# A two-layer diffusion block on one core: a running maximum spread to all partitions through DRAM, and two pieces of work moved to later steps

## The chip, the cores and the metric

The kernel runs on one core of a Trainium2 chip. The metric is the device time of one execution in microseconds; the number given for a kernel is the median of its runs. The profile is one further execution recorded by the hardware profiler. [...]

## What is computed

Two layers work on 256 latent tokens and 256 context tokens of width 1024, all in float32. Layer 0 mixes tokens with a convolution module (a depthwise convolution of 31 taps between two pointwise products), layer 1 with a bidirectional mLSTM of 4 heads of width 512. Each is followed by a squared-ReLU MLP of width 4096, and each sublayer ends in a layer norm of `ALPHA*x + gate*F(x*(1+scale)+shift)`. Only the latent tokens are the output. What matters here of the mLSTM is how its weights are made stable:

```python
bcum = jnp.cumsum(lfc, axis=-1)
dlog = bcum[..., :, None] - bcum[..., None, :] + ic[..., None, :]
dlog = jnp.where(lower, dlog, -jnp.inf)
inter = bcum + m[..., None]
m_row = jnp.maximum(inter, jnp.max(dlog, axis=-1))
scores = jnp.einsum('bhtd,bhsd->bhts', qc, kc) * jnp.exp(dlog - m_row[..., None])
...
den = jnp.sum(scores, axis=-1) + w_inter * jnp.einsum('bhtd,bhd->bht', qc, n)
h = num / jnp.maximum(jnp.abs(den), jnp.exp(-m_row))[..., None]
```

The kernel doesn't scan over chunks: it writes the whole as attention over the 512 tokens, with weights `exp(a_s + negm_t) * S`, where `a = i - bcum` and `negm` is minus the running maximum of `a`.

## The kernel before, in words

One program, written in a framework that takes instructions in program order, gives earlier ones priority, simulates the engines and from that fixes the order on each engine and queue, with all semaphores. `tc.issue_after(x)` puts what is traced in its block behind instruction x on the same engine. A tile of a tag with n buffers waits until the oldest tile of that tag has been read for the last time.

Products of weights and activations are done in three matmuls, with both operands split into a high and a low part (`mm3` and `mm3t`, lines 179 to 213). Weights come by DMA into one of three buffers `raw` (`raw_load`, line 141, on SP's queue) and are split by ScalarE (line 149, `wh`) and VectorE (line 150, `wl`) into a ring of `NW` = 4 blocks. Results of products lie in PSUM tiles, in rings by tag: "mm" 3, "ln" 2, "cv" 2, "fl" 1.

Three places are touched.

**The convolution (layer 0).** Columns of `pw1` come out one output at a time (`pw1_next`, line 900, called behind the product of output m). The depthwise convolution of 128 tokens is done as a product with a Fourier table (`fwd`, line 817), products with the transformed taps on VectorE (`products`, lines 843 and 844, into tiles `F`, a ring of 5) and an inverse transform of eight matmuls (`back`, line 854), whose result VectorE adds up with a bias (861) and takes statistics of (862). `whole` (line 809) does all three for one block of tokens; for blocks 2 and 3 it is called at outputs m = 4 and 5, behind the epilogue `pw1_epi` of that output, which ends in four transposes (line 801).

**The end of layer 0's MLP.** The last of four pieces of the second product is done in two passes over the columns of 256 tokens, the latent ones (s = 1) first. Its epilogue `e2` scales a result and adds it to the residual (line 1071, which frees the product's PSUM bank), and calls `feed0(m, s)` (line 1108), which feeds a layer norm. When the eighth part of a pass is in, the norm is finished, and for s = 1 all eight items of `u1_half` (line 1120) are traced at once: each item applies the norm (lines 577 and 578, VectorE), then scale and shift into a high part and a copy (line 600, two on ScalarE) and the low part (line 601, VectorE). The second pass (s = 0) comes behind that. The items' results are first used by the product with `up_z`.

**The mLSTM's heads (layer 1).** `Z.att` (line 44) says how steps of generators are mixed: a main chain (`o0` is the output gate of head 0, 16 steps of 12 matmuls) and a side chain, of which so many steps are taken for each step of the main one. `G0` is `decay` (line 1348): gate sums, their running maximum (the scan at line 1404) as rows `negm` of 36 partitions x 256, two transposes of it on TensorE (line 1410) and from these `guard`, the lower bound of the denominator (lines 1412 and 1414). `W0` to `W3` are `weights` (line 1450), one per head: for each direction d a matmul with a selecting matrix spreads one row of `negm` to all 128 partitions in a PSUM bank "ln" (line 1458); exponentials (lines 1466 and 1472, ScalarE), masks (1470), products with the scores (1473) and sums (1482, 1484) on VectorE give `pw` and `es`. `A0` to `A3` (`attend`) multiply them with the values; before head h's first result is used, `denominators` (line 1488) sums `es` on TensorE (1493) and reads `guard`.

Of the kernel before, what the change touches and what calls it, by code (L numbers as in the profile page):

```python
# [8 lines left out]
F32 = mybir.dt.float32  # L9
# [5 lines left out]
P = 128  # L15
D = 1024
# [15 lines left out]
class Z:  # L32
# [8 lines left out]
    pipeS = 1  # L41
    apsum = 'mm'
    dpsum = 'mm'
    att = [['o0', 'G0 W0 W1', 2], ['o1', 'A0 W2', 1.6], ['o2', 'A1 W3 D0', 2.1], ['o3', 'A2 V3', 1], ['D1 E3 D2', 'A3', 3], ['D3', '', 0]]

# [23 lines left out]
def hybrid_kernel(ctx: ExitStack, tc: tile.TileContext, xT, vecs_d, wdw_d, ada0_w, ada_w, wg_d, pw1a, pw1, pw2, w1_0, w2_0,  # L71
# [28 lines left out]
    def psum(tag="mm"):  # L100
        return pp.tile([P, 512], F32, tag=tag, name=nm(tag), bufs={"mm": 3, "ln": 2, "fl": 1, "cv": 2}[tag])
# [704 lines left out]
            for tt in range(2):  # L806
                whole(tt, [psum() for _ in range(2)])

    def whole(tt, xfs):
        fwd(0, tt, xfs)  # L810
        products(0, tt)
        products(0, tt)
        back(0, tt, psum("cv"))

    ps_ = {}

# [30 lines left out]
    def back(h, tt, o):  # L847
        sl = slice(h * 512, (h + 1) * 512)
        for i, g_ in enumerate((G1, G2)):
            for b in (0, 1):  # L850
                r = 64 * b

                def inv():
                    return nc.tensor.matmul(o[r:r + 64, :], g_[:, r:r + 64], ps_[tt][0][b][i], start=i == 0, stop=i == 1,  # L854
                                            tile_position=(0, r))
                if b == 0:
                    lead = inv()
                else:
                    with tc.issue_after(lead.ins):
                        inv()  # L860
        nc.vector.tensor_tensor(Y[tt][h], o, bdw[:, sl], op=ALU.add)
        nc.vector.bn_stats(bst[:, tt, h, :], Y[tt][h])
# [37 lines left out]
    def pw1_next(m, ps):  # L900
        if m == 3:
            first.extend(ada_load(0, 4))
            ada_g1.mm(first, range(4))
        if m == 11:
            ada_s2.mm(half + ada_load(0, 6 + ada_s2.n, halves=(1,)))
            with tc.issue_after(mark["gate"]):
                nc.scalar.activation(warm, eps, AF.Silu)
        pw1_epi(m + KO0, ps)
        if m in (1, 2):
            taps(m - 1)  # L910
        if m in (4, 6, 8):
            unit = ada_g1 if m == 4 else ada_s2
            blocks = ada_load(0, unit.u0 + unit.n)
            with tc.issue_after(lastmm[0]):
                unit.mm(blocks)
        if m in (4, 5):
            whole(m - 2, [psum(), psum("ln")])
        if m == 5:
            ada_g1.end()
        if m == 8:  # L920
            for i, tag in enumerate("SLSL"):
                half.append(tmp(tag))
                nc.sync.dma_start(half[i], ada_w[0, 6 + ada_s2.n, 0, :, i * 512:(i + 1) * 512])
        if m == 10:
            pw2_raw.extend(raw_load(pw2[g, 0]) for g in range(2))
# [175 lines left out]
            ada_n1.step()  # L1101

    lns = norm_pair(maker(hp, "ln", 3))
    cab1, u1 = [], {}

    AGAIN = [4, 5, 6, 7, 0, 1, 2, 3]

    def feed0(m, s):
        sl = HALVES[s][1]
        lns[s].feed(x[m][:, sl])  # L1110
        if len(lns[s].ts) == DT:
            lns[s].finish()
            if not cab1:
                ada_n1.flush()
                cab1.extend(comb(1, "ln2_g0", "ln2_b0", "sc1", "sh1"))
            if s == 1:
                for _ in u1_half(s):
                    pass

    def u1_half(s):  # L1120
        for i in range(DT):
# [215 lines left out]
    def gcol(d, h):  # L1337
        return 32 * d + h
# [4 lines left out]
    make_lower_triangular(nc, lower)  # L1343
    acol = con.tile([P, 4, NG], F32, name="acol")
    negm = con.tile([NG, C], F32, name="negm")
    guard = con.tile([P, 2, NG], F32, name="guard")

    def decay(_):
        gT = tmp("L")
        nc.scalar.copy(gT, gps)  # L1350
        yield
        gk = psum("ln")
        for b in range(4):
            nc.tensor.matmul(gk[:, b * 16:(b + 1) * 16], gT[:, b * P:(b + 1) * P], foldg, start=True, stop=True)
        gs = tmp("S")[:, 0:64].rearrange("p (b c) -> p b c", b=4)
        nc.vector.tensor_tensor(gs, gk[:, 0:64].rearrange("p (b c) -> p b c", b=4),
                                VA("b_gate").rearrange("p (b c) -> p b c", b=4), op=ALU.add)
        gb_ = [tmp("L"), tmp("E"), tmp("E")]
        g8 = [gb_[i // 3][:, (i % 3) * 4 * NG:(i % 3 + 1) * 4 * NG].rearrange("p (b c) -> p b c", b=4) for i in range(8)]
        ig, fg, bsb, ex, up1, cor, lf, fa = g8  # L1360
        nc.vector.memset(ig, 0.0)
        nc.vector.memset(fg, 0.0)
        for d in range(2):
            nc.vector.tensor_copy(ig[:, :, 32 * d:32 * d + 4], gs[:, :, 8 * d:8 * d + 4])
            nc.vector.tensor_copy(fg[:, :, 32 * d:32 * d + 4], gs[:, :, 8 * d + 4:8 * d + 8])


        nc.vector.scalar_tensor_tensor(fa, fg, -1.0, fg, op0=ALU.mult, op1=ALU.max)
        nc.scalar.activation(ex, fa, AF.Exp, scale=-1.0)
        nc.vector.tensor_scalar(up1, ex, 1.0, None, op0=ALU.add)  # L1370
        nc.vector.scalar_tensor_tensor(cor, up1, -1.0, ex, op0=ALU.add, op1=ALU.subtract)
        nc.scalar.activation(lf, up1, AF.Ln)
        nc.vector.reciprocal(up1, up1)
        nc.vector.tensor_tensor(cor, cor, up1, op=ALU.mult)
        nc.vector.tensor_tensor(lf, cor, lf, op=ALU.subtract)
        nc.vector.tensor_scalar(fa, fg, 0.0, None, op0=ALU.min)
        nc.vector.tensor_tensor(lf, lf, fa, op=ALU.add)

        nc.vector.memset(up1, 0.0)
        for d, (b0, b1, b2, b3) in ((0, (0, 1, 2, 3)), (1, (1, 0, 3, 2))):  # L1380
            c = slice(32 * d, 32 if d == 0 else NG)
            nc.vector.tensor_copy(up1[:, b1, c], lf[:, b0, c])
            nc.vector.tensor_tensor(up1[:, b2, c], up1[:, b1, c], lf[:, b1, c], op=ALU.add)
            nc.vector.tensor_tensor(up1[:, b3, c], up1[:, b2, c], lf[:, b2, c], op=ALU.add)
        yield
        yield
        bps = psum("ln")
        for d, cum in ((0, upper), (1, lower)):
            c = slice(32 * d, 32 if d == 0 else NG)
            reg = bps[:, 0:4 * NG].rearrange("p (b c) -> p b c", b=4)[:, :, c]  # L1390
            nc.tensor.matmul(reg, cum, lf[:, :, c], start=True, stop=False)
            nc.tensor.matmul(reg, ones, up1[:, :, c], start=False, stop=True)
        nc.vector.tensor_copy(bsb, bps[:, 0:4 * NG].rearrange("p (b c) -> p b c", b=4))
        nc.vector.tensor_tensor(acol, ig, bsb, op=ALU.subtract)

        yield
        aT = psum("ln")
        for b in range(4):
            nc.tensor.transpose(aT[:NG, b * P:(b + 1) * P], acol[:, b, :], ident)
        aR, mR = tmp("S"), tmp("S")  # L1400
        nc.vector.tensor_copy(aR[:32, :], aT[:32, :])
        nc.vector.tensor_copy(aR[32:NG, LO], aT[32:NG, LO])
        nc.vector.tensor_copy(aR[32:NG, HI], aT[32:NG, T - 1:C - 1:-1])
        nc.vector.tensor_tensor_scan(mR[:NG, :], aR[:NG, :], aR[:NG, :], 0.0, op0=ALU.max, op1=ALU.max)
        nc.vector.tensor_scalar(negm[:32, :], mR[:32, HI], -1.0, None, op0=ALU.mult)
        nc.vector.tensor_scalar(negm[32:NG, :], mR[32:NG, T - 1:C - 1:-1], -1.0, None, op0=ALU.mult)
        yield
        mT = psum("ln")
        for t in range(2):
            nc.tensor.transpose(mT[:, t * NG:(t + 1) * NG], negm[:, t * P:(t + 1) * P], ident[:NG, :NG])  # L1410
        yield
        nc.vector.tensor_tensor(guard, mT[:, 0:2 * NG].rearrange("p (t c) -> p t c", t=2), bsb[:, 2:4, :],
                                op=ALU.subtract)
        nc.scalar.activation(guard, guard, AF.Exp)
# [12 lines left out]
    close_pool()  # L1427
    close_pool()
    qe = open_pool("qe")
    sel = {d * 4 + h: ident[:NG, gcol(d, h):gcol(d, h) + 1].broadcast_to([NG, P]) for d in range(2) for h in range(H)}  # L1430
    mask = qe.tile([P, 2, 2, P], F32, name="mask")
    nc.gpsimd.memset(mask, 0.0)
    nc.gpsimd.tensor_scalar(mask[:, 0, 0, :], upper, -1.0, -NEG, op0=ALU.add, op1=ALU.mult)
# [16 lines left out]
    def weights(h):  # L1450


        es = tmp("F").rearrange("p (d t) -> p d t", d=2) if h % 2 else ES()
        short = PW(F32R)
        for d in range(2):
            cidx = gcol(d, h)
            nb = psum("ln")
            nc.tensor.matmul(nb[:, :C], sel[d * 4 + h], negm, start=True, stop=True)
            yield
            for i, b in enumerate(blocks[d]):  # L1460
                q0, q1 = rng[d, b]
# [233 lines left out]

    def chain(names):
        for n_ in names.split():
            yield from dict(G=decay, W=weights, o=gate_o, V=values, A=attend, D=down, E=early)[n_[0]](int(n_[1]))

    for main, side, per in Z.att:  # L1700
        side = chain(side)
# [268 lines left out]
```

## Time and profile before

| | before |
|---|---|
| median of 3 runs | 1683.69 us (1683.51 to 1685.66) |
| the profiled execution | 1685.65 us, span 1683.9 us |
| granted TensorE clock, mean | 0.998 |
| busy: DVE, ACT, POOL | 61%, 44%, 1% |
| HBM read, written | 283.32 MB, 15.73 MB |

How to read it: the span runs from the first to the last recorded instruction; the profiled execution's own time is 1.75 us longer. Busy shares are averages over the whole span. A matmul's recorded time includes part of its pipeline, so the distance from one start to the next tells what it costs. The chain that ended last follows from the last instruction back what released each.

### The profile page before, as it was taken

What the parts mean: (1) busy time and instruction counts of PE and PEld (TensorE: products, weight loads), DVE (VectorE), ACT (ScalarE), POOL (GpSimd) and SP (SyncE); (2) the same over time, 40 slices, a digit from 0 to 9 for tenths busy, and PEclk for the clock granted to TensorE, in tenths of its full rate; (3) what the DMA queues carried; (4) which work ended last, traced back from release to release, by engine and by line L of the source; (5) the groups of instructions that cost most, each with busy time, mean ns of one, the idle gap of its engine ahead of it and who ended that gap; (6) DMA issues with size and microseconds to landing.
All of it is one profiled execution on the core that took longest, in us unless ns stands there. A gap on an engine that the chain in (4) does not pass through costs nothing.

```text
span 1683.9 us, 22944 instructions
## 1 busy us (share of the span) xinstructions
PE 1670.1 (99%) x8960; PEld 1371.5 (81%) x8960; DVE 1035.3 (61%) x1877; ACT 743.3 (44%) x1197; POOL 14.3 (1%) x64
## 2 busy tenths in 40 slices
PE   9999999999999999999999999999999999999998
PEld 6665898888888998877788899888878878878887
DVE  6555895666635766752143653564478785786677
ACT  4313573232324476652243533442466564555453
POOL 0000000000000000000000000000000000000001
PEclk9999999999999999999999999999999999999999
DMA  9547223444324065556775752455454555675552
GB/s 357 192 150 273 86 75 113 150 137 139 138 100 150 15 200 181 184 192 250 264 257 175 254 183 104 156 188 176 145 191 174 199 216 195 247 282 184 192 180 96
DMA packets 71835, 300.53 MB, mean 178 GB/s; under 512 B 7282, under 2 KB 22386, under 8 KB 41648
## 3 DMA queue, kind: packets, MB, share of 16 engines
q1 hardware_dynamic: 54064, 284.39, 47.7%
q10 hardware_dynamic: 17664, 14.69, 2.6%
q8 instruction: 70, 1.15, 0.3%
q14 instruction: 37, 0.30, 0.1%
HBM read 283.32 MB, written 15.73 MB: 178 GB/s over the span
## 4 chain that ended last, share of the span: by engine, by line
PE 96%; DVE 3%; DMA 1%; issue 0%; ACT 0%; SPq 0%; DVEq 0%
PE mm L180 17%; PE mm L183 17%; PE mm L184 17%; PE mm L195 7%; PE mm L213 4%; PE mm L211 4%; PE mm L212 4%; PE mm L196 4%; PE cv L211 2%; PE cv L212 2%; PE cv L213 2%; PE fl L342 1%; PE cv L854 1%; PE ln L180 1%; PE fl L772 1%; PE ln L183 1%
## 5 line engine op out<-in xcount | busy, mean ns | idle before, releaser
L150 DVE TENSOR_TENSOR wl<-raw,wh 128x1024 fp32r<-128x1024 f32 x344 | 419.0, 1222 | 270.6 <-ACT wh L149 253.4
L149 ACT CAST wh<-raw 128x1024 fp32r<-128x1024 f32 x344 | 358.9, 1051 | 504.1 <-PE mm L183 270.4
L183 PE MATMUL mm<-u,wh 128*128 128x512 f32 (+1 forms) x808 | 292.1, 362 | 0.3 <-DVE u L610 0.2
L180 PE MATMUL mm<-u,wh 128*128 128x512 f32 (+1 forms) x680 | 244.3, 360 | 0.0
L184 PE MATMUL mm<-u,wl 128*128 128x512 f32 (+1 forms) x680 | 241.8, 356 | 0.0
L183 PEld LDWEIGHTS mm<-u,wh 128*128 128x128 f32 x808 | 152.6, 189 | 23.8 <-issue 1.5
L180 PEld LDWEIGHTS mm<-u,wh 128*128 128x128 f32 x680 | 128.4, 189 | 27.4 <-issue 8.8
L184 PEld LDWEIGHTS mm<-u,wl 128*128 128x128 f32 x680 | 128.5, 189 | 18.9 <-issue 1.2
L211 PE MATMUL mm<-wh,xl 128*128 128x512 f32 x256 | 101.5, 397 | 0.0
L212 PE MATMUL mm<-wh,xl 128*128 128x512 f32 x256 | 101.2, 395 | 0.0
L180 PE MATMUL mm<-xm,wh 128*128 128x512 f32 x256 | 101.0, 395 | 0.0
L213 PE MATMUL mm<-wl,xl 128*128 128x512 f32 x256 | 99.9, 395 | 0.2 <-DVE wl L150 0.2
L184 PE MATMUL mm<-xm,wl 128*128 128x512 f32 x256 | 99.7, 390 | 0.0
L180 PE MATMUL mm<-hid,wh 128*128 128x512 f32 (+1 forms) x256 | 93.3, 364 | 1.1 <-DVE x L1071 1.1
L184 PE MATMUL mm<-hid,wl 128*128 128x512 f32 (+1 forms) x256 | 92.8, 363 | 0.0
L183 PE MATMUL mm<-hid,wh 128*128 128x512 f32 (+1 forms) x256 | 92.8, 363 | 0.0
L195 PE MATMUL mm<-x,wh 128*128 128x512 f32 x232 | 81.1, 398 | 0.0
L425 DVE SCALAR_TENSOR_TENSOR S<-ar,cs,S 128x512 f32<-128x512 f32 x56 | 40.8, 749 | 61.1 <-DMA ar<-ada_w 60.9
L183 PE MATMUL mm<-qq,wh 128*128 128x272 f32 x256 | 73.9, 289 | 0.0
L180 PE MATMUL mm<-qq,wh 128*128 128x272 f32 x256 | 73.5, 289 | 0.0
L184 PE MATMUL mm<-qq,wl 128*128 128x272 f32 x256 | 73.5, 288 | 0.0
L195 PE MATMUL mm<-u,wh 128*128 128x512 f32 x192 | 68.7, 399 | 0.0
(535 smaller groups left out, 3278.0 us busy)
## 6 DMA issues: line engine op xcount, KB each, us to landing
raw<-w SPq DMA_DIRECT2D x64, 1024.0 KB, 4.8
raw<-wo SPq DMA_DIRECT2D x32, 1024.0 KB, 4.8
raw<-ada_w SPq DMA_DIRECT2D x24, 1024.0 KB, 6.4
ar<-ada_w SPq DMA_DIRECT2D x80, 256.0 KB, 3.3
raw<-wv SPq DMA_DIRECT2D x16, 1024.0 KB, 6.6
raw<-wqT SPq DMA_DIRECT2D x16, 1024.0 KB, 5.9
raw<-wq SPq DMA_DIRECT2D x16, 1024.0 KB, 5.3
raw<-wk SPq DMA_DIRECT2D x16, 1024.0 KB, 5.1
```

The lines of the kernel that those rows point to most:

```text
L149: c = nc.scalar.copy(hi, src)
L150: lastsub[0] = nc.vector.tensor_tensor(lo, src, hi.bitcast(F32), op=ALU.subtract).ins
L180: a = nc.tensor.matmul(ps, wh, xh, start=start, stop=False)
L183: nc.tensor.matmul(ps, wh, xl, start=False, stop=False)
L184: lastmm[0] = nc.tensor.matmul(ps, wl, xh, start=False, stop=stop).ins
L195: todo = [lambda s_, e_: nc.tensor.matmul(ps, wh, r[0], start=s_, stop=e_), lambda s_, e_: nc.tensor.matmul(ps[:, :n], wl, r[0][:, :n], st ...
L196: lambda s_, e_: nc.tensor.matmul(ps[:, :n], wl, r[0][:, :n], start=s_, stop=e_)]
L211: nc.tensor.matmul(ps, xh, wh, start=start, stop=False)
L212: nc.tensor.matmul(ps, xl, wh, start=False, stop=False)
L213: nc.tensor.matmul(ps, xh, wl, start=False, stop=stop)
L342: a = mark_unit[0] = nc.tensor.matmul(ps[32 * j:32 * j + 32], cs[:, kt, 14 - 2 * v:46 - 2 * v], blocks[kt], start=first and kt < 4, stop=l ...
L425: nc.vector.scalar_tensor_tensor(a, w, c, a, op0=ALU.mult, op1=ALU.add)
```

## The change

`decay` stores `negm` to a DRAM tile and ends there; what follows (transposes and `guard`) becomes a step `T0` of its own, between `W0` and `W1`. `weights` reads a row of it back, broadcast to 128 partitions, into a tile of tag "L" (a ring of 2), by one DMA per direction on SP's queue, in place of the matmul. Blocks 2 and 3 of the convolution do `back` one output later, behind that output's last matmul and ahead of its epilogue. The eight items of `u1_half(1)` are taken two at a time behind each of the first four `feed0(m, 0)`.

```diff
-    att = [['o0', 'G0 W0 W1', 2], ['o1', 'A0 W2', 1.6], ...
+    att = [['o0', 'G0 W0 T0 W1', 2], ['o1', 'A0 W2', 1.6], ...
...
-    def whole(tt, xfs):
+    def whole(tt, xfs, wait=False):
         fwd(0, tt, xfs)
         products(0, tt)
         products(0, tt)
-        back(0, tt, psum("cv"))
+        if not wait:
+            back(0, tt, psum("cv"))
...
+        if m in (5, 6):
+            with tc.issue_after(lastmm[0]):
+                back(0, m - 3, psum("cv"))
         pw1_epi(m + KO0, ps)
...
         if m in (4, 5):
-            whole(m - 2, [psum(), psum("ln")])
+            whole(m - 2, [psum(), psum("ln")], True)
...
             if s == 1:
-                for _ in u1_half(s):
-                    pass
+                sides.append(u1_half(s))
+        if s == 0 and sides:
+            for _ in range(2):
+                next(sides[0], None)
...
+    ng_dr = dp.tile([NG, C], F32, name="ng_dr")
...
         nc.vector.tensor_scalar(negm[32:NG, :], mR[32:NG, T - 1:C - 1:-1], -1.0, None, op0=ALU.mult)
+        nc.scalar.dma_start(ng_dr, negm)
+        bsbs.append(bsb)
+        yield
+
+    bsbs = []
+
+    def guards(_):
+        bsb = bsbs[0]
         yield
         mT = psum("ln")
...
+        nbs = tmp("L").rearrange("p (d t) -> p d t", d=2)
         for d in range(2):
             cidx = gcol(d, h)
-            nb = psum("ln")
-            nc.tensor.matmul(nb[:, :C], sel[d * 4 + h], negm, start=True, stop=True)
+            nc.sync.dma_start(nbs[:, d, :], ng_dr[cidx:cidx + 1, :].broadcast_to([P, C]))
+        for d in range(2):
+            cidx = gcol(d, h)
+            nb = nbs[:, d, :]
             yield
```

More of the change, by code (lines that the diff above doesn't have):

```diff
@@ L43 @@
     dpsum = 'mm'
-    att = [['o0', 'G0 W0 W1', 2], ['o1', 'A0 W2', 1.6], ['o2', 'A1 W3 D0', 2.1], ['o3', 'A2 V3', 1], ['D1 E3 D2', 'A3', 3], ['D3', '', 0]]
+    att = [['o0', 'G0 W0 T0 W1', 2], ['o1', 'A0 W2', 1.6], ['o2', 'A1 W3 D0', 2.1], ['o3', 'A2 V3', 1], ['D1 E3 D2', 'A3', 3], ['D3', '', 0]]
 _VECS = [
@@ L1103, in hybrid_kernel @@
     lns = norm_pair(maker(hp, "ln", 3))
-    cab1, u1 = [], {}
+    cab1, u1, sides = [], {}, []
     AGAIN = [4, 5, 6, 7, 0, 1, 2, 3]
@@ L1429, in hybrid_kernel @@
     qe = open_pool("qe")
-    sel = {d * 4 + h: ident[:NG, gcol(d, h):gcol(d, h) + 1].broadcast_to([NG, P]) for d in range(2) for h in range(H)}
     mask = qe.tile([P, 2, 2, P], F32, name="mask")
@@ L1697, in chain @@
         for n_ in names.split():
-            yield from dict(G=decay, W=weights, o=gate_o, V=values, A=attend, D=down, E=early)[n_[0]](int(n_[1]))
+            yield from dict(G=decay, T=guards, W=weights, o=gate_o, V=values, A=attend, D=down, E=early)[n_[0]](int(n_[1]))
     for main, side, per in Z.att:
```

## The prediction

> **What bounds the kernel now.** I read the page first: busy shares, then the chain that ended last. TensorE is busy all the time and nearly the whole chain is matmuls, so a change pays only where it takes work off TensorE, a wait from ahead of it, or lets its clock run.
>
> ```profile
> PE 1670.1 (99%) x8960; PEld 1371.5 (81%) x8960; DVE 1035.3 (61%) x1877; ACT 743.3 (44%) x1197; POOL 14.3 (1%) x64
> ...
> PE 96%; DVE 3%; DMA 1%; issue 0%; ACT 0%; SPq 0%; DVEq 0%
> ```
>
> Second, the waits of TensorE alone. The list is short, and three of its rows are places that the diff edits: L1071 (the epilogue whose result frees a product's buffer), L854 (the inverse transforms), L1410 (transposes of the running maximum).
>
> ```profile
> PE mm L180 <- DVE x L1071: 1.1, 1, 1.1
> ...
> PE cv L854 <- DVE F L843: 0.8, 3, 0.4
> PE ln L1410 <- DVE negm L1406: 0.6, 1, 0.6
> ```
>
> Third, the 16 matmuls at L1458, which the diff deletes, and a piece of the chain around one pair of them.
>
> ```profile
> L1458 PE MATMUL ln<-negm,ident x16: 376/418/479, 1241.1 to 1359.0; 36*128 36x256 f32 x16
> ...
> 1250.52 0.23 PE mm L211
> 1250.75 0.62 PE ln L1458 x2
> 1251.37 0.43 PE mm L212
> ```
>
> One call on line 1458 shows as two matmuls, so 16 records are eight pairs. The reader is to see more than 0.62: the matmul behind the pair also takes 0.43 where the one ahead of it took 0.23, so a pair costs TensorE 0.62 + 0.20 = 0.82 us. Fourth, three equal stretches around the first pairs; the columns are busy time of PE, PEld, DVE, ACT and POOL, then the granted clock, the DMA share and GB/s.
>
> ```profile
> 1240.00:1243.40 3.40, 2.78 (x12) 1.42 (x11) 2.74 (x6) 3.36 (x5) 0.00 (x0) 1.00 0.10 39
> 1243.40:1246.80 3.40, 3.40 (x10) 2.68 (x9) 1.98 (x6) 3.35 (x7) 0.00 (x0) 0.53 0.94 320
> 1246.80:1250.20 3.40, 3.40 (x16) 2.77 (x15) 2.44 (x7) 3.39 (x7) 0.00 (x0) 0.97 0.07 27
> ```
>
> In the first, TensorE is busy 2.78 of 3.40 us (it waits for the maximum, and does small matmuls of 36 rows); in the second its clock is 0.53, with 10 matmuls where the third has 16. A short wait is paid twice here: once itself, once in the clock behind it.
>
> **Part A, the running maximum through DRAM.** Removed: eight pairs. Six stand alone among the output gate's matmuls: 6 x 0.82 = 4.9 us. The first two lie in the disturbed stretch, which I cost as a whole:
>
> ```profile
> 1239.92 0.39 PE L213 MATMUL mm<-wl,xl 128*128 128x512 f32 x1
> 1240.93 0.28 PE L1410 MATMUL ln<-ident,negm 36*128 36x36 f32 x2 [0.62 <-DVE negm L1406]
> 1241.05 0.68 PE L1458 MATMUL ln<-negm,ident 36*128 36x256 f32 x2
> 1241.66 0.50 PE L211 MATMUL mm<-wh,xl 128*128 128x512 f32 x1
> ...
> 1247.16 0.40 PE L212 MATMUL mm<-wh,xl 128*128 128x512 f32 x1
> ...
> 1239.61 0.69 DVE L1530 TENSOR_TENSOR og<-mm,bo 128x512 f32<-128x512 f32 x1
> ...
> 1240.51 0.28 DVE L1406 TENSOR_SCALAR negm<-S 4x256 f32<-4x256 f32 x1
> ```
>
> The matmul of 1239.92 gives way at 1240.15 (0.23 later), and 13 gate matmuls run from 1241.66 to 1247.16. Without L1410 and L1458 ahead of them, the next limit is their product's buffer, free when the add of 1239.61 ends at 1240.30. Then 13 x 0.23 = 3.0 us at full clock end at 1243.3: 3.85 us earlier. Of these about 1.7 are the clock (3.4 us at 0.53), the rest the two pairs, the wait and the transposes.
>
> The transposes come back after head 0's weights: 2 transposes, one subtraction and one exponential. The maximum is then long there; their price on TensorE is 0.28 by their row plus the 0.20 of the matmul behind: 0.5 us back. The exponential stays behind others of its kind on ScalarE, the subtraction is 0.2 us on VectorE; both lie beside gate matmuls.
>
> Added: one store of 36 KB on ScalarE's queue and 16 broadcast loads of 128 KB on SP's. No row has this shape; the nearest are these (KB each, median us to landing):
>
> ```profile
> xl_dr<-pad ACTq DMA_DIRECT2D x16, 128.0 KB, 2.6
> ...
> bo<-bo_d SPq DMA_DIRECT2D x8, 256.0 KB, 3.5
> ```
>
> The maximum is complete at 1240.8 (L1406, above). Store 0.3 to issue and 2.6 to land, two loads 0.6 and 3.5: head 0's row lies in SBUF at 1247.8, where the first exponential now starts at 1243.24. That is 4.6 us late, and I must see who notices:
>
> ```profile
> 1243.24 0.82 ACT L1466 ACTIVATE S<-ln,acol 128x256 f32<-128x256 f32 x2
> 1244.08 1.28 ACT L1531 ACT_TABLE_LOAD   x1
> ...
> 1246.63 1.28 ACT L1472 ACT_TABLE_LOAD   x1
> 1247.92 0.62 ACT L1472 ACTIVATE S<-S 128x256 f32<-128x256 f32 x2
> ...
> 1263.31 0.28 DVE L150 TENSOR_TENSOR pw<-S,pw 128x128 fp32r<-128x128 f32 x1
> ...
> 1270.53 0.95 PE L1493 MATMUL ln<-ones,es 128*128 128x1 f32 x8
> ...
> 1313.29 0.95 PE L1493 MATMUL ln<-ones,F 128*128 128x1 f32 x8
> ```
>
> Head 0's last weight piece is split at 1263.6, and its denominators (L1493) run on TensorE at 1270.5: 7 us of slack. But TensorE now comes 3.85 + 2 x 0.82 = 5.5 us earlier, at 1265.0. Head 0 is ready between 1263.6 (the lateness is made good: between 1244 and 1248 ScalarE loads tables back and forth, and with the exponentials after both sigmoids two loads of 1.28 go) and 1268.2 (none is). So the new wait is 0 to 3.2 us; no row lets it fall below nothing, as nothing else waits for the deleted matmuls. I take 1.0, in the lower half, for the two loads are rows of this trace and the planner can put gate matmuls ahead. Behind a waiting TensorE stands all of its work, so this wait is paid in full.
>
> The Trainium skill puts a price on such small transfers: "SBUF — State Buffer", section "The DMA setup-cost knee", gives every transfer some 2 us that don't depend on its size, and its bytes at 436 GB/s on top. By that, an estimate from the page, store and load land after 2.1 and 2.3 us, 1.7 us less than by the two rows above, and the sum would be 1.0 us better, without a wait; this trace has 2.6 and 3.5 us for the nearest rows, and those decide.
>
> The later heads' loads are requested a whole head ahead: they need only a free buffer of two, the pairs of heads 2 and 3 now run at 1300 to 1359, and head 1's weights are unneeded before 1313 (its L1493, above). I cost them at nothing; without that cover each would bring the 3.5 us of a landing. Queues: the store waits on ScalarE ahead of the second sigmoid, which feeds nothing on TensorE for 25 us. The loads stand on SP ahead of gate weight loads, which is the slower rival below. Exponentials and mask adds now read SBUF; at most 0.06 us each, off the path. Part A: 4.9 + 3.85 - 0.5 - 1.0 = 7.25 us, between 5.05 and 8.25.
>
> **Part B, inverse transforms an output later.** Eight matmuls, an add and a statistics step each of outputs 2 and 3 move; no DMA does.
>
> ```profile
> 95.76 1.94 PE L854 MATMUL cv<-F,tab 128*64 128x512 f32 x8 [0.38 <-DVE F L843]
> ...
> 101.84 0.95 PE L350 MATMUL fl<-fold,F 128*128 128x4 f32 x8
> 102.85 0.65 PE L801 MATMUL ln<-ident,E 128*128 128x128 f32 x4
> ...
> 106.53 0.65 PE L854 MATMUL cv<-F,tab 128*64 128x512 f32 x2 [0.16 <-DVE F L843]
> ...
> 104.59 0.69 DVE L843 TENSOR_TENSOR F<-ln,Hc 128x512 f32<-128x512 f32 x1
> ```
>
> At their new place, behind the last matmul of the next output, the products are 6 us old: 0.38 + 0.16 = 0.54 us of waits go. They then stand beside other small matmuls (L350, L801), so up to two of the 0.20 us turns go too: 0.5 to 0.9, I take 0.7. One cost: output 3's four products need buffers of a ring of five that output 2 now holds until its inverse ends near 103.7 (101.84, where L350 now starts, + 1.9); they start at 104.59 now, so nothing, and at most 0.7 (one product) if that cover is gone. Part B: 0.7 us, between -0.2 and 0.9.
>
> **Part C, the second half in steps.** Eight items of two VectorE steps, two on ScalarE and one subtraction are now all planned ahead of the epilogues of the other half:
>
> ```profile
> 568.68 0.42 DVE L577 TENSOR_TENSOR x<-x,ln 128x256 f32<-128x256 f32 x1 [1.28 <-PE ln L571]
> ...
> 576.38 0.47 DVE L1071 SCALAR_TENSOR_TENSOR x<-mm,ada,x 128x256 f32<-128x256 f32 x1
> ...
> 576.91 0.39 PE L180 MATMUL mm<-hid,wh 128*128 128x256 f32 x1 [1.08 <-DVE x L1071]
> ...
> 589.39 0.28 PE L180 MATMUL mm<-u,wh 128*128 128x256 f32 x1
> ```
>
> VectorE runs items from 568.7 to 576.4 while three products wait, and TensorE stops for 1.08 us. With two items after each epilogue the epilogue goes first. Its 24 steps less the last few take 7.7 us, 0.33 each; two items are 6 x 0.33 = 2.0 us, and epilogue and sum 2 x 0.47: 2.9 in all. A product is 24 matmuls of half the columns, 24 x 0.115 = 2.8 us of TensorE. It just fits, and the items are only needed when the next weight matrix starts at 589.4. Gain 1.1, at worst 0.
>
> **Sum.** 7.25 + 0.7 + 1.1 = 9.05 us. The profiled execution took 1685.65 for a span of 1683.9, 2 us over the median of the runs (1683.69); the difference carries over, so the median goes to **1674.6 us**, 0.5% faster. All bounds together: gain 4.85 to 10.25, that is 1673.4 to 1678.8.
>
> **Rivals.** (1) **Head 0 comes late**: the DRAM trip takes the place of the removed wait. For it: SBUF at 1247.8 against 1243.24, and TensorE early. Against it: 7 us of slack, two table loads gone. Price: 3.2 instead of 1.0, and a clock stretch behind it again (1.7): gain 5.15, 1678.5.
> (2) **The slow clock stays.** If the stretch at 0.53 doesn't come from the wait and the small matmuls, it only moves: 1.7 us less, 1676.3. Against it: it begins right behind the stretch with TensorE busy 82%, and is over one stretch later. The Trainium skill speaks for this rival: "TensorE: Matmul & The Clock Gate", Part 1 on the HAM clock gate, lets the clock drop after an idle window of about 3.4 us. The row's 0.62 us is no such window, so by that rule the drop has another cause and stays.
> (3) **Steps without effect**: the planner orders VectorE's work in B and C as before, or puts other work ahead. 1.8 us less: 1676.4. Against it: each wait names the very step that moves.
> (4) **SP is held, slower than before.** Head 1's broadcast takes the buffer that the guard's subtraction reads last, and that now comes after head 0. If the planner puts this load on SP early, SP stops there with gate weight loads behind it. That SP can wait in place is a row:
>
> ```profile
> L1440 SPq EVENT_SEMAPHORE  x12: 17/17/2660, 1209.4 to 1494.1; - x12
> ...
> raw<-wo SPq DMA_DIRECT2D x32, 1024.0 KB, 4.8
> ```
>
> TensorE lives on the four split weight blocks meanwhile (12 matmuls each), 48 x 0.23 = 11.0 us, and the load behind needs 4.8 to land. A hold of H costs H + 4.8 - 11.0; it eats the gain of 9.05 from H = 15 us, and makes the kernel slower by over 0.2% from 18.7. From the store's landing (1243.7) to head 0's end (1268.2 at the latest) it could be 24.5: 18.3 - 9.05 = 9.25 us slower, 1692.9. Against it: the longest such wait now is 2.66 us, and the planner sends loads by when they can go.
>
> **How the numbers follow.** Forecast 0.60, (1) 0.15, (2) 0.07, (3) 0.06, (4) beyond 18.7 us 0.06, (4) with a hold about 15 us or (1) doubled 0.06. A measurement of this kernel can tell about 0.2%, 3.4 us, from no change. Faster: 0.60 + 0.15 + 0.07 + 0.06 = 0.88; same 0.06; slower 0.06. The range goes from 1671.5 (the lower bound and 2 us for turns and waits that I don't see) to 1680.0 (rival 1 with another 1.5 us, just short of the 0.2% line).
>
> **What would show it.** A: no L1458; the windows behind 1240 at clock 1.00; no wait at L1410's successor; L1493 of head 0 about 5 us earlier, with or without a wait for the last split or the denominators' sum. B: no L854 row for outputs 2 and 3 in TensorE's waits. C: no wait for L1071. VectorE's load in the heads' stage, third number:
>
> ```profile
> 1300.00:1400.00 100.00, 100.00 (x446) 80.85 (x447) 79.51 (x134) 63.86 (x91) 0.00 (x0) 1.00 0.57 199
> ```
>
> Wrong would make me: TensorE waiting for weight splits between 1240 and 1270 (SP held), a clock below 1.00 elsewhere, or VectorE, busy 79.51 of 100 us in that stage, becoming the one that TensorE waits for.

## The result, and the profile after

| | before | after |
|---|---|---|
| median | 1683.69 us (5 runs, 1683.51 to 1685.66) | 1676.25 us (5 runs, 1675.70 to 1676.78) |
| the profiled execution | 1685.65, span 1683.9 | 1676.15, span 1674.3 |

The ratio is 0.9954 (95% interval 0.9939 to 0.9968): 7.4 us less, where the prediction said 9.05, and 1676.25 where it said 1674.6. The two profiled executions differ by 9.6 us of span, about as predicted. So the question is not only what the change did, but why 9.6 us between two profiles are 7.4 between two medians.

The page of after first, its busy shares and its chain. In these views PE is TensorE (PEld its weight loads), DVE VectorE, ACT ScalarE, POOL GpSimd and SP SyncE. TensorE still carries nearly all of the chain; 16 matmuls fewer are the eight pairs.

```profile
PE 1662.7 (99%) x8944; PEld 1369.3 (82%) x8944; DVE 1034.4 (62%) x1877; ACT 742.5 (44%) x1196; POOL 14.3 (1%) x64
...
PE 95%; DVE 2%; DMA 1%; ACT 0%; issue 0%; SPq 0%; DVEq 0%; ACTq 0%
```

TensorE's waits in after (line waited at, releaser, us in total, times, longest). The rows for the product's buffer and for the transposed maximum are gone, the inverse transforms (L855 now) keep 0.3 of 0.8; the second row is new.

```profile
PE cv L174 <- DVE ones L128: 1.1, 1, 1.1
PE mm L211 <- ACT wh L149: 0.8, 1, 0.8
PE ln L801 <- DVE E L798: 0.3, 1, 0.3
PE mm L213 <- DVE wl L150: 0.3, 1, 0.3
PE cv L855 <- DVE F L844: 0.3, 1, 0.3
PE fl L342 <- DMA raw<-ada_w: 0.2, 1, 0.2
PE mm L183 <- DVE u L610: 0.2, 1, 0.2
```

Three equal stretches of after from 1237 us on (columns as in the prediction). TensorE is busy 3.33 of 3.40 us in the first, and its clock stays at 1.00.

```profile
1237.00:1240.40 3.40, 3.33 (x15) 2.18 (x14) 3.15 (x7) 3.35 (x5) 0.00 (x0) 1.00 0.09 32
1240.40:1243.80 3.40, 3.40 (x16) 2.77 (x16) 1.39 (x2) 2.85 (x4) 0.00 (x0) 1.00 0.90 287
1243.80:1247.20 3.40, 3.40 (x17) 2.81 (x16) 2.40 (x3) 1.94 (x4) 0.00 (x0) 1.00 0.83 237
```

And the way of the maximum in after's timeline: complete, stored, loaded for heads 0 and 1, first use on VectorE and ScalarE, last split of head 0, its denominators. The last three lines are ScalarE's table loads ahead of head 0, for the sigmoids (L1548) and for the guard's exponential (L1429), and that exponential.

```profile
1237.95 0.28 DVE L1413 TENSOR_SCALAR negm<-S 4x256 f32<-4x256 f32 x1
1238.26 0.55 ACTq L1414 DMA_DIRECT2D ng_dr<-negm  x1
1240.53 2.00 SPq L1472 DMA_DIRECT2D L<-ng_dr  x4
1245.80 0.48 DVE L1487 SCALAR_TENSOR_TENSOR S<-L,acol,mask 128x256 f32<-128x256 f32 x1 [0.94 <-DMA L<-ng_dr]
1246.22 0.90 ACT L1483 ACTIVATE S<-L,acol 128x256 f32<-128x256 f32 x2
1258.25 0.28 DVE L150 TENSOR_TENSOR pw<-S,pw 128x128 fp32r<-128x128 f32 x1
1264.83 0.95 PE L1510 MATMUL ln<-ones,es 128*128 128x1 f32 x8
...
1237.25 1.28 ACT L1548 ACT_TABLE_LOAD   x1
...
1239.71 1.28 ACT L1429 ACT_TABLE_LOAD   x1
1241.01 0.26 ACT L1429 ACTIVATE guard<-guard 128x72 f32<-128x72 f32 x1
```

Head 0 starts later than before (1246.22 against 1243.24) and ends earlier (1258.5 against 1263.6). TensorE reaches the denominators 6.3 us after that and waits for nothing.

To lay profiles beside one another I count from the first matmul of L801, which starts between 45.8 and 46.3 us from one execution to another: that difference arises at the start of an execution and not by the change. Starts in us after it, in before, in one more profile of before (e1, below) and in after, where the last three rows are lines 1406, 1609 and 1808:

| | before | before again | after |
|---|---|---|---|
| last L801 (end of B's stage) | 100.9 | 100.9 | 99.7 |
| first L772 (behind C's stage) | 696.5 | 696.5 | 694.1 |
| L1399, transposes ahead of the maximum | 1188.9 | 1188.6 | 1186.3 |
| last L1592, end of the heads' stage | 1425.8 | 1424.0 | 1416.1 |
| first L1791, last stage | 1517.4 | 1515.6 | 1507.7 |

B gives 1.2 and C another 1.2 (2.4 at L772). A, from L1399 to L1791, gives 7.1 against the first profile of before and 5.6 against the second. Against the second all three make 7.9 at L1791; the spans differ by 7.4, since after's execution reached the first L801 0.5 later.

### The profile page after: what moved, and what is told of

Same layout as the page of the kernel before. It is cut to its first block, busy times and chain, and to the rows that moved or that the text cites. A ratio compares the mean times of both kernels' runs of the same rounds, so it can differ in the third digit from the quotient of the medians.

```text
span 1674.3 us, 22935 instructions
## 1 busy us (share of the span) xinstructions
PE 1662.7 (99%) x8944; PEld 1369.3 (82%) x8944; DVE 1034.4 (62%) x1877; ACT 742.5 (44%) x1196; POOL 14.3 (1%) x64
## 4 chain that ended last, share of the span: by engine, by line
PE 95%; DVE 2%; DMA 1%; ACT 0%; issue 0%; SPq 0%; DVEq 0%; ACTq 0%
PE mm L180 17%; PE mm L184 17%; PE mm L183 17%; PE mm L195 7%; PE mm L211 4%; PE mm L213 4%; PE mm L196 4%; PE mm L212 4%; PE cv L211 1%; PE cv L213 1%; PE cv L212 1%; PE fl L342 1%; PE ln L180 1%; PE cv L855 1%; PE fl L772 1%; PE ln L183 1%
## 5 line engine op out<-in xcount | busy, mean ns | idle before, releaser
L184 PE MATMUL mm<-xm,wl 128*128 128x512 f32 x256 | 99.7, 390 | 0.0
```

The source lines that it names most:

```text
L184: lastmm[0] = nc.tensor.matmul(ps, wl, xh, start=False, stop=stop).ins
```

## Experiments

**Theory:** the profiled execution of before holds a stretch of half clock (1.7 us) that most executions of before don't have; the median gains only what is left. **Rival:** the half clock belongs to the kernel before, and the missing 2 us are somewhere else. A second question is the DRAM trip: the prediction gave it a wait of 1.0 us, and TensorE had none; was there slack, and how much? Ratios below are to the kernel before on the same chip, with the 95% interval.

**e1, the kernel before once more**, and its parts alone: **e2** with part A, **e3** with B, **e4** with C, each with the hunks of the diff above that belong to it.

> The kernel before, once more, unchanged. The profiled execution of before took 1685.65 us and has a stretch with the granted clock at 0.53; the other four runs of before lie at 1683.5 to 1683.9. Theory (the 2 us over the median are that stretch of half clock, which only some executions have): most runs at 1683.5 to 1684.0, a profile of such a run has a span near 1682.0, and its TensorE clock stays at 1.00 between 1235 and 1255, with the wait at L1410 still there (0.6). Rival (every execution has the half clock there, and the 2 us are somewhere else): a profile near 1682.0 still has the 3.4 us at about 0.5.

> Before with part A alone (running maximum through DRAM, transposes later). Theory: against the typical run of before the selecting matmuls and the wait give 5.0 to 5.5 us, the clock stretch nothing or little, so about 1678.4 (ratio 0.9968). Rival (the stretch of half clock belongs to every execution of before): 7.2 us, 1676.5 (ratio 0.9957).

> Before with part B alone (two inverse transforms an output later). By the landmark at the end of the modulated outputs, 147.1 in before and 146.0 in after: gain 1.1, about 1682.6. By the prediction's sum: 0.7, 1683.0. If the gain were given back at the next buffer or weight load: 1683.7. No clock change is expected in any of them.

> Before with part C alone (second half's items in steps of two). By the landmark at the last epilogue (597.3 against 596.0 with B's 1.1 in it) the gain is 0.2 at that point, and 2.4 less 1.1 = 1.3 from the first product behind it on: about 1682.4 if the wait at L1071 (1.08) goes whole, 1683.7 if a later wait takes it back.

| | median (range) | ratio |
|---|---|---|
| e1, before again | 1683.69 (1683.27 to 1685.77) | 1.0002 (0.9994 to 1.0011) |
| e2, A alone | 1678.26 (1678.00 to 1678.46) | 0.9967 (0.9955 to 0.9979) |
| e3, B alone | 1682.40 (1682.01 to 1684.02) | 0.9994 (0.9985 to 1.0003) |
| e4, C alone | 1683.15 (1682.09 to 1684.22) | 0.9996 (0.9988 to 1.0005) |

The profile of e1 is one of 1683.38 us. Its stretch with the wait for the maximum and the one behind it:

```profile
1239.40:1242.80 3.40, 2.77 (x12) 1.49 (x11) 2.67 (x6) 3.36 (x5) 0.00 (x0) 1.00 0.15 50
1242.80:1246.20 3.40, 3.40 (x16) 2.77 (x16) 2.05 (x6) 3.35 (x7) 0.00 (x0) 1.00 0.99 319
```

TensorE is busy 2.77 us in the first, as in the first profile (2.78), and waits the same 0.6 at L1410; yet the stretch behind it has 16 matmuls at clock 1.00 where the other had 10 at 0.53. The span is 1681.7, 2.2 less: 1.8 by the table's row behind the heads (0.3 of them already at L1399, by a wait at L1391 that e1 doesn't have; 1.5 in the stage with the half clock), 0.4 by the start. Of e1's 11 runs eight lie between 1683.27 and 1683.93 and three between 1685.16 and 1685.77. **So the theory holds:** the same program, the same wait, and the half clock only in some executions. (That the three longer runs are those with it is inferred from their times; only profiled executions show the clock by stretches.) B alone shows the like: eight runs at 1682.01 to 1682.43, three at 1683.68 to 1684.02, and the one profiled is among the three; it has the half clock at the same place:

```profile
1237.90:1241.30 3.40, 2.78 (x12) 1.35 (x11) 2.90 (x6) 3.36 (x4) 0.00 (x0) 1.00 0.15 34
1241.30:1244.70 3.40, 3.40 (x9) 2.61 (x9) 1.82 (x5) 3.35 (x8) 0.00 (x0) 0.51 0.98 293
```

A alone is 5.4 under before (1683.62 in these rounds) with runs within 0.5 us: the theory's 5.0 to 5.5, not the rival's 7.2. B's 1.2 agrees with its landmark, though its interval just takes in 1. C alone gives only 0.5 in the median, but its eleven runs spread over 2.1 us: five lie at 1682.09 to 1682.80, and six, with the median and the profiled run (1683.51), at 1683.15 to 1684.22. The profiled one has no half clock; it has 1.3 at L772, and behind L1791 its span is 121.3 us long where e1's is 120.3. A new wait there takes half of this:

```profile
PE ln L212 <- DVE hid L150: 0.5, 1, 0.5
```

That says what this execution gave back. The five lower runs, with 1682.34 in their middle, are 1.3 under before; what sets them apart no profile shows. Nor does it say whether C gives anything back in the changed kernel; for this:

**e9, after without C** (the lines of `sides` taken back), **and e11, after once more.**

> The changed kernel without part C (A and B only). Theory (C is worth the whole wait at L1071, 1.1 to 1.3, and C alone showed only 0.5 because its profile lost 1.0 again in the last stage, behind 1560): 1677.5. Rival (C is worth 0.5, as alone): 1676.8.

> The changed kernel once more, unchanged, as the measure for the other three. All theories: 1676.3, no run 1.7 above the others, TensorE's clock at 1.00 from 1235 to 1280, and the wait of 0.75 at 1425.

e9: 1677.30 (1676.67 to 1677.68), ratio 0.9958 (0.9944 to 0.9971); e11: 1676.11 (1675.66 to 1676.50), 0.9951 (0.9939 to 0.9964). C is worth 1.2 in the changed kernel, and the row it removes stands in e9 again:

```profile
PE mm L180 <- DVE x L1075: 1.1, 1, 1.1
```

e11's clock is 1.00 from 1235 to 1280, and no run of the ten of e11 and after is more than 1.2 above the lowest.

**e5, the pairs kept**, all else as in after:

```diff
+    sel = {d * 4 + h: ident[:NG, gcol(d, h):gcol(d, h) + 1].broadcast_to([NG, P]) for d in range(2) for h in range(H)}
...
-            nb = nbs[:, d, :]
+            nb = psum("ln")
+            nc.tensor.matmul(nb[:, :C], sel[d * 4 + h], negm, start=True, stop=True)
```

> The changed kernel, but the maximum spread by the eight selecting matmuls as before, no DRAM trip; the transposes stay later, B and C stay. Theory (the pairs cost 0.82 each and the wait for the maximum 0.6, since the first pair now stands behind it): 8 x 0.82 + 0.6 - 0.2 slower than after, about 1683.2 less the two matmul turns that the first two pairs share, so 1682.0 to 1683.2; and as wait and small matmuls are back, a part of its runs is 1.7 longer. Rival (the pairs cost only their own 0.62 and the gain of A comes from the transposes' new place): 8 x 0.42 = 3.4 slower, 1679.6.

1681.56 (1681.18 to 1682.43), ratio 0.9985 (0.9976 to 0.9994): 5.3 slower than after, between the two theories and nearer to the first. TensorE waits for the maximum again, and not at the cast that after waits for:

```profile
PE ln L1471 <- DVE negm L1412: 0.6, 1, 0.6
```

5.3 - 0.6 + 0.8 = 5.5 for eight pairs: 0.69 each, an estimate from these two waits. In e5's own chain a pair that stands alone still costs 0.62 + 0.20 = 0.82, six times, and the two of head 0, which stand together and share their turn, 1.10 + 0.20: 6.2 for the eight. The 0.7 between the two sums is not placed. No run is 1.7 above the others, though wait and small matmuls are there: that part of the expectation fell.

**e6, the transposes first**: DRAM trip and all else as in after, but the transposes, the subtraction and the exponential back in `decay`.

```diff
-    att = [['o0', 'G0 W0 T0 W1', 2], ...
+    att = [['o0', 'G0 W0 W1', 2], ...
...
         nc.scalar.dma_start(ng_dr, negm)
-        bsbs.append(bsb)
-        yield
-
-    bsbs = []
-
-    def guards(_):
-        bsb = bsbs[0]
         yield
         mT = psum("ln")
```

> The changed kernel with the two transposes, the subtraction and the exponential back where they stood in before, right behind the maximum (TensorE waits there again, by the order of its instructions); the DRAM trip and the missing pairs stay. Theory (most of A is the pairs, and the transposes' place is worth the wait of 0.6): 1676.8. Rival a (wait and transposes alone make the half clock in some runs): a part of the runs at 1678.5. Rival b (the exponential ahead of head 0's brings back the table loads and makes head 0 late): 1.3 to 2.6 more, 1678 to 1679.5, with a TensorE wait at the denominators or the first attention product.

1679.44 (1678.95 to 1679.69), ratio 0.9970 (0.9959 to 0.9982): 3.2 slower than after. Rival b. ScalarE in e6 up to head 0's first exponential:

```profile
1236.61 1.28 ACT L1541 ACT_TABLE_LOAD   x1
...
1238.55 1.28 ACT L1422 ACT_TABLE_LOAD   x1
...
1240.11 1.28 ACT L1541 ACT_TABLE_LOAD   x1
...
1245.96 1.28 ACT L1476 ACT_TABLE_LOAD   x1
1247.26 0.91 ACT L1476 ACTIVATE S<-L,acol 128x256 f32<-128x256 f32 x2
```

The guard's exponential goes between two sigmoids, and four table loads come ahead of head 0. In after the transposes stand six matmuls later, the exponential comes behind both sigmoids (1241.01), two of the loads are gone, and head 0 starts 1.0 us earlier. What e6 loses shows in TensorE's waits below (after has 0.8 of the first row, and none of the others): not at head 0's results, but at the transposes themselves, at weight blocks, and at an addition that has to free a buffer. That the two table loads more, 2.6 us, make these late is argued from the order on ScalarE; no run takes them out alone.

```profile
PE mm L211 <- ACT wh L149: 2.0, 2, 1.3
...
PE ln L1418 <- DVE negm L1413: 0.6, 1, 0.6
PE mm L211 <- DVE og L1540: 0.6, 1, 0.6
```

**e7, a second hop**: the maximum is copied once more from DRAM to DRAM before the loads read it.

```diff
-        nc.scalar.dma_start(ng_dr, negm)
+        nc.scalar.dma_start(ng_d1, negm)
+        nc.gpsimd.dma_start(ng_dr, ng_d1)
```

> The changed kernel with the maximum copied once more from DRAM to DRAM on GpSimd's queue before the loads read it, so that head 0's row comes later by one more DMA (2.6 to 4.7 us by the rows of small transfers), and SP, whose two loads wait for it in place, is held as long. Theory (in the changed kernel head 0's last split ended at 1258.5 and its denominators ran at 1264.8, 6.3 us of slack): no change, 1676.3. The prediction's step (1.0 us of wait already at the trip as it is, and each further us paid in full): 2.6 to 4.7 slower, 1679 to 1681. Its fourth rival (a hold H of SP costs H + 4.8 - 11): nothing below 6 us.

1683.61 (1683.37 to 1684.37), ratio 0.9997 (0.9988 to 1.0006): the whole gain is gone, 7.4 us, more than any of the three had. My theory of 6.3 us of slack fell. Head 0 starts 2.6 us later than in after (1248.79 against 1246.22), and TensorE waits behind it. Its timeline, with the addition on VectorE and the cast on ScalarE that it waits for:

```profile
1248.79 0.91 ACT L1485 ACTIVATE S<-L,acol 128x256 f32<-128x256 f32 x2 [2.86 <-DMA L<-ng_dr]
...
1260.67 0.68 DVE L1549 TENSOR_TENSOR og<-mm,bo 128x512 f32<-128x512 f32 x1
...
1261.41 0.50 PE L211 MATMUL mm<-wh,xl 128*128 128x512 f32 x1 [1.43 <-DVE og L1549]
...
1265.34 0.95 PE L1512 MATMUL ln<-ones,es 128*128 128x1 f32 x8
...
1270.80 1.03 ACT L149 CAST wh<-raw 128x1024 fp32r<-128x1024 f32 x1
...
1271.88 0.50 PE L211 MATMUL mm<-wh,xl 128*128 128x512 f32 x1 [2.77 <-ACT wh L149]
```

The denominators (L1512) run without a wait at 1265.34: head 0 itself is in time, as the slack said. Late is what stands behind it on VectorE and ScalarE, which take their work in order: the addition of the output gate, and the cast of the next weight block. The chain of e7 runs from 1250.5 to 1273.2 through these two engines alone, pieces of heads 0 and 1 and four table loads, without one matmul. None of TensorE's waits there is for a DMA, so SP, which sent nothing between 1240.1 and 1245.33, cost nothing that shows: its hold of 5.2 us was within what the fourth rival allows. The second wait is followed by a stretch of half clock:

```profile
1269.90:1273.30 3.40, 1.23 (x5) 0.70 (x5) 3.37 (x9) 3.40 (x9) 0.00 (x0) 0.99 0.00 0
1273.30:1276.70 3.40, 3.40 (x8) 2.72 (x9) 3.40 (x12) 1.13 (x4) 0.00 (x0) 0.51 0.66 234
```

1.4 + 2.8 + 1.7 of clock (an estimate, 3.4 us at half clock) are 5.9 of the 7.4 us; the rest I have not placed.

**e8, a longer wait** in the kernel before: the scan repeated twice.

```diff
+        nc.vector.tensor_tensor_scan(aR[:NG, :], mR[:NG, :], mR[:NG, :], 0.0, op0=ALU.max, op1=ALU.max)
+        nc.vector.tensor_tensor_scan(mR[:NG, :], aR[:NG, :], aR[:NG, :], 0.0, op0=ALU.max, op1=ALU.max)
         nc.vector.tensor_scalar(negm[:32, :], mR[:32, HI], -1.0, None, op0=ALU.mult)
```

> The kernel before with the scan of the maximum repeated twice (it changes no value), 1.21 us each on VectorE, so that the maximum is complete 2.4 us later; the order puts 13 gate matmuls (3.0 us) ahead of the transposes instead of waiting. Theory (the wait of 0.62 is what it costs, and wait with small matmuls is what sets off the half clock): wait gone, so 0.5 faster than before, 1683.1, and no run 1.7 above the others. Rival (the transposes and selecting matmuls alone set it off): still about a quarter of the runs 1.7 longer. Rival (the later maximum delays head 0): slower by up to 2.4.

1687.43 (1686.05 to 1690.81), ratio 1.0021 (1.0012 to 1.0030). The wait didn't go: it is 1.3 now, in spite of the 13 matmuls ahead of it, so this run can't tell wait from small matmuls. Seven of its 11 runs lie at 1686.05 to 1687.52 and four at 1689.36 to 1690.81. The lower group, too, is some 2.7 slower than before (1686.32 in its middle against 1683.61), so the last expectation, a later maximum that delays what stands behind it, came nearest. The profiled run (1689.63) is of the upper group. It has a second new wait, 0.7 for a weight cast behind 1250, and two stretches of half clock behind the first:

```profile
PE ln L1412 <- DVE negm L1408: 1.3, 1, 1.3
...
1243.40:1246.80 3.40, 2.10 (x10) 1.43 (x9) 3.09 (x7) 2.49 (x5) 0.00 (x0) 0.93 0.63 174
1246.80:1250.20 3.40, 3.40 (x8) 1.92 (x7) 3.15 (x7) 1.98 (x4) 0.00 (x0) 0.50 0.44 186
1250.20:1253.60 3.40, 3.40 (x10) 2.64 (x10) 0.78 (x3) 0.10 (x1) 0.00 (x0) 0.57 0.86 308
```

**e10 and e12, the wait that after gained.** In after's chain of waits a weight load asked for at 1418.20 is late, and with it a cast and TensorE:

```profile
1416.94 1.24 DVE wl L150
...
1418.20 6.03 DMA raw<-wo
...
1424.32 1.06 ACT wh L149
```

The load waits for a buffer that the split at 1416.94 reads last. e10 writes the last head's values ahead of the third head's attention, e12 takes the side work 1.3 times as densely:

```diff
-    att = [..., ['o3', 'A2 V3', 1], ...
+    att = [..., ['o3', 'V3 A2', 1], ...
```

```diff
-    att = [..., ['o3', 'A2 V3', 1], ...
+    att = [..., ['o3', 'A2 V3', 1.3], ...
```

> The changed kernel with the last head's values loaded ahead of the third head's attention instead of behind it. The changed kernel has one TensorE wait left that before hadn't: 0.75 us at 1425.4 for a weight cast whose load was requested late (1418.2, when a buffer of the ring of three came free). Theory (the order of that load in the ring makes it): wait gone, 1675.5. Rival (the cast is late because ScalarE is, or another wait comes in its place): 1676.3 or more.

> The changed kernel with the work beside the last output gate taken 1.3 times as densely, so that the third head's attention and the last head's values come earlier among the gate's matmuls. Theory (VectorE and ScalarE, in their order, make the cast at 1425 late; earlier side work makes room): 1675.5. Rival (they are full in that stage and the wait moves): 1676.3 to 1677.5.

e10: 1675.00 (1674.31 to 1675.21), ratio 0.9944 (0.9931 to 0.9956); e12: 1674.99 (1674.69 to 1676.02), 0.9945 (0.9933 to 0.9958). On the same chip after (e11) has 1676.11, so both gain 1.1, a little more than the wait (1.0 in e11), and none of e10's five runs reaches the lowest of e11's. These are all of e10's waits:

```profile
PE cv L174 <- DVE ones L128: 1.1, 1, 1.1
PE ln L801 <- DVE E L798: 0.3, 1, 0.3
PE cv L855 <- DVE F L844: 0.3, 1, 0.3
PE mm L183 <- DVE u L610: 0.2, 1, 0.2
PE mm L213 <- DVE wl L150: 0.2, 1, 0.2
```

Both ways remove the wait, so it doesn't hang on one load's place alone; which of the two causes (the ring, or the order of ScalarE's and VectorE's work) is the first they don't tell.

## Why the prediction came out as it did

**Sum, "the difference carries over": wrong, and this is the step that missed.** Profile against profile the change gives 9.6 us where the sum said 9.05. But the profiled execution of before has 2.2 us more span than e1's: 1.5 in the stage with the half clock (1.7 was said), 0.3 ahead of it and 0.4 at the start. Most executions, and with them the median, don't have the half clock, so A's term, which counted it, could not be taken from the median. With the 1.7 left out, the sum is 7.35, against 7.4 between the medians. That it fits so closely is in part luck: against e1's profile the parts make 7.9, mostly because B gave 0.5 more than was said, and after's later start takes 0.5 back. The sign was there to read in the prediction itself: it noted the 2 us and did not ask where in the profile they were.

**Part A: right in size, for partly other reasons.** 7.25 was said, 7.1 is there against the profile with the half clock; without it 5.55 was said, and 5.6 is there (5.4 for A alone, e2). The parts differ: the pairs leave 0.69 each over all eight (e5), though the six that stand alone cost 0.82 in its chain, as said; the wait for head 0, 1.0, is not there; a wait of 0.8 that I did not have came at 1425 (e10 and e12 show that it can go).

**Head 0's lateness: the trip was right, the slack was asked of the wrong engine.** The trip took 7.6 us from the complete maximum to the first use, 7.0 were said. The loads land later than by the row taken:

```profile
L<-ng_dr SPq DMA_DIRECT2D x8, 128.0 KB, 4.7
```

The Trainium skill, "SBUF — State Buffer", section "The DMA setup-cost knee", gave 2.3 us for such a load as an estimate; here it took 4.7, twice that, and 1.2 more than the row of the nearest shape. The lateness was made good as the text allowed: two table loads up to the end of head 0's first exponentials in place of four. But the 7 us between last split and denominators were not the slack. e7 made head 0 2.6 us later and lost everything, while the denominators did not wait at all: the slack that counts is that of the addition and the weight cast behind head 0's work on VectorE and ScalarE.

**The transposes: price right on TensorE, place and effect on ScalarE missed.** They do not come back after head 0's weights. In after they run at 1239.39, six matmuls later than in e6, and cost 0.45 by the starts around them. The guard's subtraction follows at 1240.00 and its exponential at 1241.01, 5 us ahead of head 0's first. Leaving them right behind the maximum costs 3.2 us (e6): 0.6 by TensorE's own wait, the rest, as argued there, by two table loads. I counted the new place only as a cost of 0.5; with the DRAM trip it is worth 3.2.

**Part B: too small.** 1.2 for 0.7, above its bound of 0.9. The waits went as said (0.8 to 0.3). In after's timeline the group stands against other small matmuls (and the second one too, at 109.50):

```profile
99.43 1.94 PE L855 MATMUL cv<-F,tab 128*64 128x512 f32 x8
101.30 0.66 PE L801 MATMUL ln<-ident,E 128*128 128x128 f32 x4
```

So two turns of 0.20 can have gone beside the 0.5 of waits; the rest, 0.3, is not placed.

**Part C: right.** 1.2 for 1.1 (e9 against e11); alone it gives part of this back in the last stage, in the execution that was profiled (e4). The sum that said "it just fits" had 2.9 us on VectorE for 2.8 on TensorE, which does not quite fit; the wait went all the same.

**The rivals.** (1) did not come, but e7 shows it real, with the clock stretch behind it, and dearer than I had it: 2.6 us more of lateness cost 7.4, and not 2.6 and 1.7 for the clock. (2), that the half clock stays, would have given nearly the measured time for a reason that is not the case: after has no half clock. The rule that spoke for it, in the Trainium skill's "TensorE: Matmul & The Clock Gate", Part 1, asks for an idle window of some 3.4 us before the clock drops. The profiles have drops of that length behind waits of 0.6, 1.3 and 2.8 us, none with an idle stretch of 3.4 ahead of it; what the same Part says of the window, that it runs free of the kernel's start, fits that the same wait is followed by a drop in one execution and by none in another. (3) fell with the waits gone. (4) did not arise: the order put the guard's subtraction (1240.00) ahead of all loads, and SP had the four of them out in 2.0 us from 1240.53.

## What to carry to other kernels

Before you subtract a gain from a median, ask whether the profiled execution is one like the median's: a difference of 2 us has a place in the trace, and a term that lies in that place must not be counted again. Slack on an engine that works in order is not the time until its result is used, but the time until the next thing queued behind it is used; look up what stands behind the late piece. A latency that is moved off the busiest engine is only free as long as the engines beside it have room in that stage: here 2.6 us more of lateness cost all of the 7.4.

## What the runs showed of the hardware

TensorE's clock drops to about half in whole stretches of 3.4 us (0.51 to 0.53 in before, e3 and e7; two of them, 0.50 and 0.57, in e8). They begin between 2.8 us (e8) and 4.1 us (e7) behind the beginning of a wait of 0.6 us or more; with a wait of 0.6, before has such a stretch in one profiled execution and not in the other. Not every wait is followed by one: e6's 1.3 and after's 0.75 have none behind them, and of e5's 11 runs none is 1.7 longer. What decides, beside the wait, is open. Behind the last matmul of the program, too, the clock falls to 0.50, in these 14 profiles between 2.2 us (e4, e7) and 5.0 us (after) after its end.

A broadcast load of 128 KB from a row of 1 KB took 4.7 us on SP's queue in the median of after and e7, and 5.3 in e6, against 2.6 to 3.9 for two other kinds of transfer of that size on ScalarE's queue. A single load of 128 KB on SP's queue (`rk`) took 3.5 to 5.8, so it is not shown that the broadcast is what makes these loads longer.
